# The scores of a chunked recurrence on TensorE, from 128-wide tiles to 32-wide blocks side by side

## The chip, the cores and the metric

The kernel runs on one core of a Trainium2 chip. The core has TensorE (PE in the profile; its loads of the stationary operand are PEld), VectorE (DVE), ScalarE (ACT), GpSimd (POOL) and SyncE (SP), which issues most of the DMAs. The metric is the device time of one execution in microseconds (us): the median of the runs shown.

## The reference, cut to what matters

One layer of a diffusion backbone works on 1024 latent and 128 context tokens: a feed-forward half step, a token mixer (attention beside a gated linear recurrence, HGRN2), and a second feed-forward half step. The recurrence has 8 heads of 64 key and 64 value channels and runs in both directions. Its score matrix is what the change is about:

```python
b = jnp.cumsum(logf.reshape(B, n, CHUNK, H, DK), axis=2)
diff = b[:, :, :, None] - b[:, :, None, :]
decay = jnp.where(mask, jnp.exp(jnp.where(mask, diff, 0.0)), 0.0)
A = jnp.einsum('bntshk,bnthk,bnshk->bnhts', decay, qc, kc)
o_intra = jnp.einsum('bnhts,bnshv->bnthv', A, vc)
```

A[t, s] is the product of query t and key s, decayed by the gates f of the tokens between them; it is multiplied with the values, and the state that comes in from earlier chunks is added. All inputs and outputs are float32.

## The kernel before, in words

The 1152 tokens (latent and context together) lie along the free dimension, in three column blocks of 384 ("chunks", `CW`), each of three 128-token tiles. The program has five stages one after the other: first feed-forward, the recurrence stage (`hgrn`, line 687), attention, the merge of both, second feed-forward. The stage in question goes from about 878 to 1526 us.

In it, two kinds of work share the engines. The first is projections (`proj_f`, `proj_q`, `proj_v`, `proj_gate`, `proj_sg`): products of the normalised input with 128 columns of `w_in`, each a sum of 24 records of 384 columns into one PSUM bank (tile `mm`, lines 451 to 453: the operands are split in a high and a low part, so each product is done three times). They depend on nothing in the scan of the head at hand. The second is the scan itself, for 8 heads by 3 chunks, 24 times:

- `scan_pre` (line 769) makes, on ScalarE, VectorE and GpSimd, decayed keys and queries within groups of 8 tokens (Kb, Qb) and over groups of 8 (KE, QP), with the products T of the gates. Partitions 0 to 63 hold the forward direction (A in the code), 64 to 127 the backward one (B).
- `scan_lev` (line 816) makes the scores. First, line 838: for each 128-token tile Kb times Qb, 64 partitions deep, once per direction, into two PSUM banks of 128 x 3 x 128. VectorE copies from them, under a mask that leaves the 8 x 8 blocks on the diagonal (forward: upper triangle, backward: lower one), into A1 and A2 (`copy_predicated`, line 839). Then four levels m = 8, 16, 32, 64: line 853 multiplies the half-zeroed keys kr with QP, 128 partitions deep, for all pairs of tokens in the 128-token tile; of these only the pairs in neighbouring blocks of m tokens are wanted. Levels 8, 16 and 32 take them with a mask into A1 (line 868), level 64 with two copies on ScalarE (lines 870 and 871). After each level's product KE and QP are multiplied in place with the neighbour's T (line 864; two of QP's halves on VectorE and GpSimd), and ScalarE makes the next half-zeroed keys (lines 844 and 845). At the end VectorE adds A1 and A2 to Af (line 875), TensorE transposes KE (kt, line 879), ScalarE copies that (kT, line 881), and one more product makes dS.
- `scan_out` (line 889), once per head, passes the state through nine tiles on VectorE (line 896) and multiplies Af with the values and QP with the states (po, lines 904 and 908).

Three PSUM banks go round for the scores (tag `lv`), three for small tiles (`sm`), two for the projections (`mm`). A masked copy writes nothing where the mask is zero, and A1 and A2 are zeroed once at the start, so outside the blocks they stay zero.

What sets the order: `hgrn` steps generators by turns. After each `yield` of the level generator one step of projection work (12 records of 384 columns) and one step of the next chunk's `scan_pre` follow, so in TensorE's queue a level's product stands, then 12 projection records, then the next level's product. Each engine works its own instructions in the fixed order that results when the kernel is built. An instruction that waits holds up all that is behind it on its engine.

A float32 product of TensorE stands in the profile as two records; a product of the split operands (fp32r) as one.

Of the kernel before, what the change touches and what calls it, by code (L numbers as in the profile page):

```python
# [9 lines left out]
F32 = mybir.dt.float32  # L10
F32R = mybir.dt.float32r
BF16 = mybir.dt.bfloat16
U8 = mybir.dt.uint8
# [6 lines left out]
P = 128  # L20
# [13 lines left out]
EPS = 1e-6  # L34
SIDE = (1, 2, 3, 4, 5, 6, 7, 8)
QKS = 96.0 ** -0.5
LB_MIN = 1e-8
QW = T // 4
QUARTERS = [(q * QW, (q + 1) * QW) for q in range(4)]
# [48 lines left out]
class Trunk:  # L88
# [494 lines left out]

    def mixer_consts(self, cp):
        nc, a = self.nc, self.a
        self.mask = cp.tile([P, 5, P], U8, name="mask")
        mf = self.tt(F32, "maskf")[:, : 5 * P]
        nc.scalar.dma_start(mf, a["mask"])
        nc.vector.tensor_copy(self.mask.rearrange("p a b -> p (a b)"), mf)
        self.onesb = cp.tile([P, P], F32, name="onesb")  # L590
        nc.vector.memset(self.onesb, 0.0)
        nc.vector.memset(self.onesb[0:64, 0:64], 1.0 / 64)
        nc.vector.memset(self.onesb[64:128, 64:128], 1.0 / 64)
        self.onesq = cp.tile([P, P], F32, name="onesq")
        nc.vector.memset(self.onesq, 1.0 / 384)
        self.onesk = cp.tile([P, P], F32, name="onesk")
        nc.vector.memset(self.onesk, 1.0 / 256)
# [89 lines left out]
    def hgrn(self):  # L687
        nc = self.nc
# [4 lines left out]
        A, B = slice(0, 64), slice(64, P)  # L693
        self.kr = {m: [f32(f"kr{m}_{i}", [P, CW]) for i in range(1)] for m in (8, 16, 32, 64)}
        self.XY = [f32(n, [P, 48, 8]) for n in "XY"]
        self.A1 = [f32(f"A1_{i}", [P, 3, P]) for i in range(2)]
        self.A2 = [f32("A2", [P, 3, P])]
        for m in self.kr:
            for t in self.kr[m]:
                nc.vector.memset(t, 0.0)  # L700
# [115 lines left out]
    def scan_lev(self, d, b):  # L816
# [8 lines left out]
            nc.sync.dma_start(S[A, 0], self.a["state"][d["h"], 0])  # L825
            nc.sync.dma_start(S[B, 7], self.a["state"][d["h"], 1])
        dS = d["dS"]
        A1, A2 = self.A1[self.cnt % 2], self.A2[0]
        self.cnt += 1
        Kb, Qb, KE, Tm = d["pre"]  # L830
        bc = lambda t, m: t.unsqueeze(2).to_broadcast([t.shape[0], t.shape[1], m])
        qp = QP[:, c0 : c0 + CW]
        lv = lambda: self.pp.tile([P, 3, P], F32, tag="lv", bufs=3, name="lv")
        mb = lambda i: self.mask[:, i].unsqueeze(1).to_broadcast([P, 3, P])
        for r, dst, mi in ((A, A1, 0), (B, A2, 1)):
            ps = lv()
            for j in range(3):
                nc.tensor.matmul(ps[:, j], Kb[r, ts(j, P)], Qb[r, ts(j, P)], start=True, stop=True)
            nc.vector.copy_predicated(dst, mb(mi), ps)
        hm = lambda t, m: t.rearrange("p (n h m) -> p n h m", h=2, m=m)  # L840

        def key_half(m):
            kr = self.kr[m][0]
            nc.scalar.copy(hm(kr, m)[A, :, 0], hm(KE, m)[A, :, 0])
            nc.scalar.copy(hm(kr, m)[B, :, 1], hm(KE, m)[B, :, 1])

        key_half(8)
        yield
        for li, m in enumerate((8, 16, 32, 64)):
            kr = self.kr[m][0]  # L850
            ps = lv()
            for j in range(3):
                nc.tensor.matmul(ps[:, j], kr[:, ts(j, P)], qp[:, ts(j, P)], start=True, stop=True)  # L853
            tv = Tm.rearrange("p (n h) -> p n h", h=2)
            tL, tR = tv[:, :, 0], tv[:, :, 1]
            Tn = Gall[:, 3 * b : 3 * b + 3] if m == 64 else tmp(f"T{2 * m}", 3, (P, CW // (2 * m)))
# [8 lines left out]
            nc.vector.tensor_mul(Tn, tL, tR)  # L865
            if m < 64:
                key_half(2 * m)
                nc.vector.copy_predicated(A1, mb(2 + li), ps)
            else:
                nc.scalar.copy(A1[A, :, B], ps[A, :, B])  # L870
                nc.scalar.copy(A1[B, :, A], ps[B, :, A])
            Tm = Tn
            yield
        Af = tmp("Af", 4, (P, 3, P))
        nc.vector.tensor_add(Af, A1, A2)
        d["As"][b] = Af
        pt = self.pp.tile([P, 3, P], F32, tag="sm", bufs=3, name="kt")
        for j in range(3):
# [870 lines left out]
def mask_table():  # L1749
    import numpy as np  # L1750

    s, t = np.arange(P)[:, None], np.arange(P)[None, :]
    same = lambda b: s // b == t // b
    m = [same(8) & (s <= t), same(8) & (s >= t)]
    m += [same(2 * b) & ~same(b) for b in (8, 16, 32)]
    return np.concatenate(m, 1).astype(np.float32)


# [33 lines left out]
```

## Time and profile before

| | |
|---|---|
| median of 3 runs | 3015.09 us (3014.46 to 3016.74) |
| profiled execution, its own time | 3016.44 us |
| its span, first to last instruction | 3014.5 us |
| mean granted TensorE clock | 0.985 |
| TensorE busy, whole span | 2901.7 us (96%) |
| recurrence stage, 878 to 1526 us: TensorE busy | 619.5 of 648 us |
| the same: VectorE busy | 479.0 us |
| the same: ScalarE busy | 338.8 us |
| the same: GpSimd busy | 202.1 us |

Rows of a group read: line, engine, operation, tile written <- tiles read, shapes, how often | busy us, mean ns of one | idle time of the engine just ahead of them, and who ended it. On TensorE a shape such as 128\*32 gives the part of the array that is used: 128 partitions deep, 32 columns wide. Rows of a timeline or a chain read: start in us, length in us, engine, line, operation. A matmul's record reaches from its issue to the end of its drain, so records overlap; the distance from start to start is what counts. A row of waits reads: engine, line, who waits <- for whom: us in total, times, longest.

### The profile page before, as it was taken

What the parts mean: (1) busy time and instruction counts of PE and PEld (TensorE: products, weight loads), DVE (VectorE), ACT (ScalarE), POOL (GpSimd) and SP (SyncE); (2) the same over time, 40 slices, a digit from 0 to 9 for tenths busy, and PEclk for the clock granted to TensorE, in tenths of its full rate; (3) what the DMA queues carried; (4) which work ended last, traced back from release to release, by engine and by line L of the source; (5) the groups of instructions that cost most, each with busy time, mean ns of one, the idle gap of its engine ahead of it and who ended that gap; (6) DMA issues with size and microseconds to landing.
All of it is one profiled execution on the core that took longest, in us unless ns stands there. A gap on an engine that the chain in (4) does not pass through costs nothing.

```text
span 3014.5 us, 49640 instructions
## 1 busy us (share of the span) xinstructions
PE 2901.7 (96%) x18630; PEld 2746.8 (91%) x18630; DVE 1998.2 (66%) x4074; ACT 1238.7 (41%) x2372; POOL 1082.1 (36%) x980
## 2 busy tenths in 40 slices
PE   7999999999989999999998999989999999999998
PEld 5999999999979989898997787669999999999997
DVE  7787777566667777878356777745674665546665
ACT  5432332221364555555245777721362323232113
POOL 3133223453253333333244444532342232236424
PEclk9999999999989999999998999999999999999999
DMA  6643333631111111111110001273352322236211
GB/s 231 204 143 121 124 124 108 247 101 59 62 58 58 38 46 37 51 37 53 58 46 12 18 16 32 63 237 105 106 185 95 101 89 78 76 102 215 90 44 63
DMA packets 148591, 281.34 MB, mean 93 GB/s; under 512 B 18880, under 2 KB 83328, under 8 KB 148352
## 3 DMA queue, kind: packets, MB, share of 16 engines
q1 hardware_dynamic: 148208, 277.85, 28.0%
q8 instruction: 147, 2.41, 0.3%
q14 instruction: 92, 0.75, 0.1%
q10 hardware_dynamic: 144, 0.33, 0.0%
HBM read 214.59 MB, written 63.52 MB: 92 GB/s over the span
## 4 chain that ended last, share of the span: by engine, by line
PE 53%; DVE 11%; ACT 4%; issue 2%; POOL 1%; DMA 1%; DVEq 0%; SPq 0%; ACTq 0%; POOLq 0%
PE b L1546 14%; PE dn L452 4%; PE dn L451 4%; PE dn L453 4%; PE mm L451 4%; PE mm L452 3%; PE mm L453 3%; PE mps L1222 1%; DVE KE L864 1%; PE lv L853 1%; PE ups L453 1%; PE ups L452 1%; PE ups L451 1%; PE sps L1263 1%; PE sps L1265 1%
## 5 line engine op out<-in xcount | busy, mean ns | idle before, releaser
L480 DVE SCALAR_TENSOR_TENSOR x<-dn,modt,x 128x256 f32<-128x256 f32 (+4 forms) x728 | 353.4, 505 | 210.6 <-PE dn L453 209.4
L1546 PE MATMUL b<-xo,wo 128*128 128x288 f32 x3552 | 485.1, 296 | 0.0
L1546 PEld LDWEIGHTS b<-xo,wo 128*128 128x128 f32 x3552 | 477.0, 188 | 0.0
L232 POOL TENSOR_TENSOR wl<-raw,wh 128x1024 fp32r<-128x1024 f32 (+3 forms) x107 | 242.3, 2265 | 371.5 <-ACT wh L231 357.3
L451 PE MATMUL mm<-xh,wh 128*128 128x384 f32 (+1 forms) x1008 | 361.9, 359 | 11.0 <-DVE q L645 8.9
L1546 PE MATMUL b<-bh,wo 128*128 128x288 f32 x1776 | 365.9, 295 | 1.1 <-ACT et L1556 1.1
L453 PE MATMUL mm<-xh,wl 128*128 128x384 f32 (+1 forms) x1008 | 343.0, 340 | 1.8 <-POOL wl L232 1.8
L452 PE MATMUL mm<-xl,wh 128*128 128x384 f32 (+1 forms) x1008 | 342.5, 340 | 0.0
L1546 PEld LDWEIGHTS b<-bh,wo 128*128 128x128 f32 x1776 | 289.2, 188 | 1.3 <-ACT et L1556 1.3
L1546 PE MATMUL b<-bl,wo 128*128 128x288 f32 x888 | 262.0, 295 | 0.0
L451 PEld LDWEIGHTS mm<-xh,wh 128*128 128x128 f32 (+1 forms) x1008 | 190.8, 189 | 20.3 <-DVE q L645 9.7
L1521 ACT CAST wo<-raw 128x512 fp32r<-128x512 f32 x185 | 114.7, 621 | 228.4 <-PE b L1546 112.8
L231 ACT CAST wh<-raw 128x1024 fp32r<-128x1024 f32 (+3 forms) x109 | 105.3, 968 | 251.0 <-PE dn L452 162.0
L451 PE MATMUL dn<-hh,wh 128*128 128x384 f32 (+2 forms) x576 | 195.9, 340 | 1.9 <-DVE et L1562 0.9
L453 PE MATMUL dn<-hh,wl 128*128 128x384 f32 (+2 forms) x576 | 194.4, 337 | 1.0 <-POOL wl L232 1.0
L452 PE MATMUL dn<-hl,wh 128*128 128x384 f32 (+2 forms) x576 | 194.5, 338 | 0.0
L1522 DVE TENSOR_TENSOR wo<-raw,wo 128x512 fp32r<-128x512 f32 x185 | 127.1, 688 | 101.4 <-ACT wo L1521 98.0
L453 PEld LDWEIGHTS mm<-xh,wl 128*128 128x128 f32 (+1 forms) x1008 | 190.4, 189 | 3.1 <-POOL wl L232 2.1
L452 PEld LDWEIGHTS mm<-xl,wh 128*128 128x128 f32 (+1 forms) x1008 | 191.2, 190 | 1.8 <-issue 0.4
L1624 POOL TENSOR_TENSOR hl<-hr,hh 128x1152 fp32r<-128x1152 f32 x44 | 118.1, 2689 | 201.3 <-ACT hh L1623 121.4
L1517 POOL TENSOR_TENSOR ws<-raw 128x256 f32<-128x256 f32 x74 | 66.2, 915 | 301.4 <-DMA raw<-in_w 277.3
L1272 POOL TENSOR_TENSOR ehl<-e,ehl 128x512 fp32r<-128x512 f32 x93 | 123.0, 1327 | 143.0 <-ACT ehl L1270 80.1
(382 smaller groups left out, 7257.0 us busy)
## 6 DMA issues: line engine op xcount, KB each, us to landing
raw<-in_w SPq DMA_DIRECT2D x148, 256.0 KB, 3.1
raw<-in_w SPq DMA_DIRECT2D x58, 512.0 KB, 3.7
hr<-hs SPq DMA_DIRECT2D x44, 576.0 KB, 5.0
hs<-et SPq DMA_DIRECT2D x148, 144.0 KB, 1.8
raw<-in_w_in SPq DMA_DIRECT2D x41, 512.0 KB, 3.6
wada<-in_w_aT SPq DMA_DIRECT2D x80, 256.0 KB, 2.8
wada<-in_w_ada SPq DMA_DIRECT2D x32, 512.0 KB, 5.8
hb<-hd SPq DMA_DIRECT2D x44, 288.0 KB, 3.5
```

What stands on the lines that cost most here:

```text
L231: pin(self.nc.scalar.copy(wh, raw))
L232: pin((eng or self.nc.gpsimd).tensor_sub(wl, raw, wh))
L451: nc.tensor.matmul(ps, wh, xh, start=start and i == 0, stop=False)
L452: nc.tensor.matmul(ps, wh, xl, start=False, stop=False)
L453: nc.tensor.matmul(ps, wl, xh, start=False, stop=stop and i == n - 1)
L480: nc.vector.scalar_tensor_tensor(self.x[m][:, a:b], ps[:, a - lo : b - lo], self.modt[:, gm, m, s : s + 1], self.x[m][:, a:b], ALU.mult, A ...
L1272: eng.tensor_sub(el, e, eh)
L1517: nc.gpsimd.tensor_tensor(o[:, c], x[:, c], y[:, c], op)
L1521: nc.scalar.copy(wh, src[i])
L1522: nc.vector.tensor_sub(wl, src[i], wh)
L1546: nc.tensor.matmul(ps, w[:, k], x[:, k, :QW], start=first, stop=last, skip_group_check=home != i)
L1624: nc.gpsimd.tensor_sub(hl, raw, hh)
```

## The change

The scores are made and masked in 32-token blocks instead of 128-token tiles.

- The first products and levels 8 and 16 are made for 32 x 32 blocks alone: key block g of tile j with query block g, with the result at partitions 32g to 32g+31 of the j-th 32 columns of a compact bank of 128 x 3 x 32. The instruction names a tile of the array by row and column (`tile_position`), so block g uses column strip g, and in the first products the two directions use the two row halves.
- The masked copies, A1, A2 and the masks shrink from 128 x 3 x 128 to 128 x 3 x 32. Level 32 has no masked copy any more. A2 gets a second buffer.
- Levels 32 and 64 go straight to their places in one full bank (128 x 3 x 128), level 32 as four 32 x 32 products per tile (block g of the keys with the neighbouring block of the queries), level 64 as two 64 x 64 products.
- The blocks on the diagonal are put into the same bank with products by the identity: for A1, then A2, and each strip g, 32 columns of the identity times all of A1 (96 columns), the second added onto the first in PSUM. One ScalarE copy of the bank makes Af, in place of two ScalarE copies and the addition on VectorE.

So per chunk 18 products of 128 columns (6 first, 12 for levels) become 24, 12, 12 and 12 of 32 columns, 6 of 64 and 8 of 96.

```diff
@@ -34,6 +34,7 @@
 EPS = 1e-6
 SIDE = (1, 2, 3, 4, 5, 6, 7, 8)
 QKS = 96.0 ** -0.5
+BK = 32
 LB_MIN = 1e-8
 QW = T // 4
 QUARTERS = [(q * QW, (q + 1) * QW) for q in range(4)]
@@ -583,8 +584,8 @@
 
     def mixer_consts(self, cp):
         nc, a = self.nc, self.a
-        self.mask = cp.tile([P, 5, P], U8, name="mask")
-        mf = self.tt(F32, "maskf")[:, : 5 * P]
+        self.mask = cp.tile([P, 4, BK], U8, name="mask")
+        mf = self.tt(F32, "maskf")[:, : 4 * BK]
         nc.scalar.dma_start(mf, a["mask"])
         nc.vector.tensor_copy(self.mask.rearrange("p a b -> p (a b)"), mf)
         self.onesb = cp.tile([P, P], F32, name="onesb")
@@ -693,8 +694,8 @@
         A, B = slice(0, 64), slice(64, P)
         self.kr = {m: [f32(f"kr{m}_{i}", [P, CW]) for i in range(1)] for m in (8, 16, 32, 64)}
         self.XY = [f32(n, [P, 48, 8]) for n in "XY"]
-        self.A1 = [f32(f"A1_{i}", [P, 3, P]) for i in range(2)]
-        self.A2 = [f32("A2", [P, 3, P])]
+        self.A1 = [f32(f"A1_{i}", [P, 3, BK]) for i in range(2)]
+        self.A2 = [f32(f"A2_{i}", [P, 3, BK]) for i in range(2)]
         for m in self.kr:
             for t in self.kr[m]:
                 nc.vector.memset(t, 0.0)
@@ -825,17 +826,27 @@
             nc.sync.dma_start(S[A, 0], self.a["state"][d["h"], 0])
             nc.sync.dma_start(S[B, 7], self.a["state"][d["h"], 1])
         dS = d["dS"]
-        A1, A2 = self.A1[self.cnt % 2], self.A2[0]
+        A1, A2 = self.A1[self.cnt % 2], self.A2[self.cnt % 2]
         self.cnt += 1
         Kb, Qb, KE, Tm = d["pre"]
         bc = lambda t, m: t.unsqueeze(2).to_broadcast([t.shape[0], t.shape[1], m])
         qp = QP[:, c0 : c0 + CW]
-        lv = lambda: self.pp.tile([P, 3, P], F32, tag="lv", bufs=3, name="lv")
-        mb = lambda i: self.mask[:, i].unsqueeze(1).to_broadcast([P, 3, P])
-        for r, dst, mi in ((A, A1, 0), (B, A2, 1)):
-            ps = lv()
-            for j in range(3):
-                nc.tensor.matmul(ps[:, j], Kb[r, ts(j, P)], Qb[r, ts(j, P)], start=True, stop=True)
+        lv = lambda n=BK: self.pp.tile([P, 3, n], F32, tag="lv", bufs=3, name="lv")
+        mb = lambda i: self.mask[:, i].unsqueeze(1).to_broadcast([P, 3, BK])
+        blk = lambda j, g, n=BK: slice(j * P + g * n, j * P + g * n + n)
+
+        def tiles(out, lhsT, rhs, row, col, start=True, stop=True):
+            nc.tensor.matmul(
+                out, lhsT, rhs, start=start, stop=stop, tile_position=(row, col), skip_group_check=True
+            )
+
+        first = lv(), lv()
+        for j in range(3):
+            for g in range(4):
+                for r, ps in zip((A, B), first):
+                    v = blk(j, g)
+                    tiles(ps[ts(g, BK), j], Kb[r, v], Qb[r, v], r.start, BK * g)
+        for ps, dst, mi in zip(first, (A1, A2), (0, 1)):
             nc.vector.copy_predicated(dst, mb(mi), ps)
         hm = lambda t, m: t.rearrange("p (n h m) -> p n h m", h=2, m=m)
 
@@ -846,11 +857,19 @@
 
         key_half(8)
         yield
+        full = None
         for li, m in enumerate((8, 16, 32, 64)):
             kr = self.kr[m][0]
-            ps = lv()
+            if m < BK:
+                ps, n, far = lv(), BK, 0
+            else:
+                ps = full = full or lv(P)
+                n, far = m, 1
             for j in range(3):
-                nc.tensor.matmul(ps[:, j], kr[:, ts(j, P)], qp[:, ts(j, P)], start=True, stop=True)
+                for g in range(P // n):
+                    q = g ^ far
+                    out = ps[ts(g, n), j] if not far else ps[ts(g, n), j, ts(q, n)]
+                    tiles(out, kr[:, blk(j, g, n)], qp[:, blk(j, q, n)], 0, n * g)
             tv = Tm.rearrange("p (n h) -> p n h", h=2)
             tL, tR = tv[:, :, 0], tv[:, :, 1]
             Tn = Gall[:, 3 * b : 3 * b + 3] if m == 64 else tmp(f"T{2 * m}", 3, (P, CW // (2 * m)))
@@ -865,14 +884,15 @@
             nc.vector.tensor_mul(Tn, tL, tR)
             if m < 64:
                 key_half(2 * m)
+            if m < BK:
                 nc.vector.copy_predicated(A1, mb(2 + li), ps)
-            else:
-                nc.scalar.copy(A1[A, :, B], ps[A, :, B])
-                nc.scalar.copy(A1[B, :, A], ps[B, :, A])
             Tm = Tn
             yield
+        for i, t in enumerate((A1, A2)):
+            for g in range(4):
+                tiles(full[ts(g, BK), :, ts(g, BK)], self.ident[:, ts(g, BK)], t, 0, BK * g, not i, bool(i))
         Af = tmp("Af", 4, (P, 3, P))
-        nc.vector.tensor_add(Af, A1, A2)
+        nc.scalar.copy(Af, full)
         d["As"][b] = Af
         pt = self.pp.tile([P, 3, P], F32, tag="sm", bufs=3, name="kt")
         for j in range(3):
@@ -1749,10 +1769,10 @@
 def mask_table():
     import numpy as np
 
-    s, t = np.arange(P)[:, None], np.arange(P)[None, :]
+    s, t = np.arange(P)[:, None] % BK, np.arange(BK)[None, :]
     same = lambda b: s // b == t // b
     m = [same(8) & (s <= t), same(8) & (s >= t)]
-    m += [same(2 * b) & ~same(b) for b in (8, 16, 32)]
+    m += [same(2 * b) & ~same(b) for b in (8, 16)]
     return np.concatenate(m, 1).astype(np.float32)
 
 
```

The order on TensorE at the end of a chunk, before: the product of level 64 (kr\_0\_8912 are that level's keys), then projection records, then the transposes kt.

```order
L853 MATMUL lv<-QP,kr_0_8912 128x128 x3
L451 MATMUL mm<-xh_8318,wh 128x384
L452 MATMUL mm<-xl_8319,wh 128x384
L453 MATMUL mm<-xh_8318,wl 128x384
L451 MATMUL mm<-xh_8320,wh 128x384
L452 MATMUL mm<-xl_8321,wh 128x384
L453 MATMUL mm<-xh_8320,wl 128x384
L879 MATMUL kt<-ident,KE 128x128 x3
L451 MATMUL mm<-xh_8322,wh 128x384
```

And after the change, the same place (A\_0\_8915 is A1, A\_0\_8917 is A2):

```order
L454 MATMUL mm<-xh_8318,wl 128x384
L452 MATMUL mm<-xh_8320,wh 128x384
L839 MATMUL lv<-QP,kr_0_8912 64x64 x6
L453 MATMUL mm<-xl_8321,wh 128x384
L454 MATMUL mm<-xh_8320,wl 128x384
L839 MATMUL lv<-A_0_8915,ident 32x3x32 x4
L839 MATMUL lv<-A_0_8917,ident 32x3x32 x4
L899 MATMUL kt<-ident,KE 128x128 x3
L452 MATMUL mm<-xh_8322,wh 128x384
```

The level's three products have become six on 64-column strips, and eight identity products stand right ahead of the transposes; the level's product stands some projection records later than it did.

The order on VectorE around levels 32 and 64 of a chunk, before (KE, QP and T as above; X, Y, TK, TQ belong to the next chunk's `scan_pre`):

```order
L645 TENSOR_TENSOR q<-mm,sg 128x384
L864 TENSOR_TENSOR QP<-QP,T_10326 64x6x32
L868 COPY_PREDICATED A_0_8915<-mask,lv 128x384
L864 TENSOR_TENSOR KE<-KE,T_10550 64x6x32 x2
L790 TENSOR_TENSOR X<-fs,X 128x48
L803 COPY TK<-Y 64x48
L806 TENSOR_TENSOR TQ<-Y,fs 64x48
L791 RECIPROCAL Y<-X 128x48x3
L864 TENSOR_TENSOR QP<-QP,T_10355 64x3x64
L875 TENSOR_TENSOR Af<-A_0_8915,A_8917 128x384
L864 TENSOR_TENSOR KE<-KE,T_10577 64x3x64 x2
```

And after the change:

```order
L883 TENSOR_TENSOR QP<-QP,T_10572 64x6x32
L646 TENSOR_TENSOR q<-mm,sg 128x384
L883 TENSOR_TENSOR KE<-KE,T_10848 64x6x32 x2
L791 TENSOR_TENSOR X<-fs,X 128x48
L804 COPY TK<-Y 64x48
L807 TENSOR_TENSOR TQ<-Y,fs 64x48
L792 RECIPROCAL Y<-X 128x48x3
L883 TENSOR_TENSOR QP<-QP,T_10610 64x3x64
L883 TENSOR_TENSOR KE<-KE,T_10884 64x3x64 x2
```

The masked copy of level 32 and the addition are gone; a step of a projection (q) stands behind the multiplication of QP where it stood ahead of it.

## The prediction

> **What bounds the kernel now.** I read the page first, then the recurrence stage alone (the stretch from 878 to 1526 us, in which every instruction of the change lies) by busy time, by groups, by waits and by the chain that ended last, and last the timeline around single bursts.
>
> The page's head, then the row of the busy-time table for that stretch (PE, PEld, VectorE, ScalarE, GpSimd, granted clock):
>
> ```profile
> span 3014.5 us, 49640 instructions
> ...
> 878.00:1526.00 648.00, 619.47 (x3883) 584.00 (x3882) 479.01 (x1050) 338.76 (x702) 202.13 (x236) 0.99 0.15 48
> ```
>
> TensorE is the bound in the stage, 619 of 648 us at a granted clock of 0.99. But 648 - 619 = 28 us are open, and the waits of TensorE and of its weight loads there say on whom (us in total, times, longest):
>
> ```profile
> PE lv L853 <- DVE QP L864: 16.9, 14, 2.3
> PE lv L853 <- POOL QP L864: 4.0, 5, 1.2
> PEld lv L853 <- POOL QP L864: 8.2, 13, 1.5
> ```
>
> After each level's score product the query copy QP is multiplied in place (VectorE and GpSimd, L864), and the next level's product needs it. These waits are 21 us on TensorE, 29 us with the weight loads. So there are two ways to gain: less work on TensorE, or an earlier QP. The chain between 1193 and 1360 us (two heads) shows when QP is late: it runs on VectorE and ScalarE from 1234 to 1275 and from 1289 to 1334, 86 of about 156 us, and on TensorE otherwise. The pieces of it that the change touches:
>
> ```profile
> 1235.31 0.59 DVE A L868
> ...
> 1242.42 0.56 DVE Af L875
> ...
> 1252.63 0.54 DVE A L839
> ...
> 1254.39 0.44 DVE A L839
> ...
> 1256.60 0.58 DVE A L868
> ...
> 1260.55 0.58 DVE A L868
> ...
> 1264.28 0.59 DVE A L868
> ...
> 1295.33 0.58 DVE A L868
> ...
> 1300.54 0.56 DVE Af L875
> ...
> 1306.21 1.06 DVE A L839 x2
> ...
> 1310.48 0.49 DVE A L868
> ...
> 1313.25 0.58 DVE A L868
> ...
> 1317.02 0.58 DVE A L868
> ...
> 1320.64 0.56 DVE Af L875
> ...
> 1327.81 0.98 DVE A L839 x2
> ```
>
> The first seven sum to 3.88 us, the other eight to 5.39: 9.3 us of chain for two heads.
>
> **The change, part by part.** Six groups of the stage carry the prices (busy us, mean ns of one):
>
> ```profile
> L853 PE MATMUL lv<-QP,kr 128*128 128x128 f32 x576 | 83.7, 282 | 21.0 <-DVE QP L864 16.9 <-POOL QP L864 4.0
> L868 DVE COPY_PREDICATED A<-mask,lv 128x384 f32<-128x384 uint8 x72 | 42.6, 592 | 2.1
> L839 DVE COPY_PREDICATED A<-mask,lv 128x384 f32<-128x384 uint8 x48 | 25.4, 577 | 68.8 <-PE lv L838 68.5
> L875 DVE TENSOR_TENSOR Af<-A,A 128x384 f32<-128x384 f32 x24 | 15.1, 629 | 1.7 <-ACT A L871 1.5
> L870 ACT COPY A<-lv 64x192 f32<-64x192 f32 x24 | 7.4, 310 | 11.6 <-PE lv L853 11.4
> L881 ACT COPY kT<-kt 128x384 f32<-128x384 f32 x24 | 11.5, 478 | 9.5 <-PE kt L879 9.4
> ```
>
> There are 24 chunks (8 heads by 3). One f32 product is two records: 24 x 4 levels x 3 = 288 products stand as x576.
>
> *VectorE.* A chunk has 2 x 0.577 + 3 x 0.592 + 0.629 = 3.56 us of masks and adding. After it has four masked copies of 96 columns. No such copy is in the trace; from below it is bounded by a two-column copy out of PSUM, from above by the 0.59 us of 384 columns:
>
> ```profile
> L167 DVE COPY bias<-pb x2: 147/153/159, 67.1 to 70.6; 128x2 f32<-128x2 f32 x2
> ```
>
> Between the two, (592 - 153)/382 = 1.15 ns a column: 0.153 + 94 x 1.15 ns = 0.26 us. I take that. So 3.56 becomes 1.04, and 2.5 us a chunk, 60 us in all, leave VectorE. If a copy cost what it costs now, 3.56 - 4 x 0.59 = 1.2 us a chunk, 29 us, would still go; at 0.153 a copy it would be 71.
>
> *ScalarE.* Two copies of 0.31 go, one of 128x384 out of PSUM comes, priced by the kT row: 0.62 becomes 0.48 us. The new copy waits for the identity products; behind it on ScalarE stands the kT copy, which waits for the transposes right behind those products anyway. So it costs nothing while that order holds, and 0.48 us a chunk, 11 us, if ScalarE were the bound. The identity products in turn wait for masks that VectorE finished two levels earlier, and the score bank that they share with levels 32 and 64 is held until that copy, with two other banks left for the next chunk's first products.
>
> *TensorE, before.* Two bursts with their neighbours:
>
> ```profile
> 1206.27 0.34 PE L453 MATMUL mm<-xh,wl 128*128 128x384 f32 x1
> 1206.45 0.83 PE L853 MATMUL lv<-QP,kr 128*128 128x128 f32 x6
> ...
> 1207.29 0.34 PE L452 MATMUL mm<-xl,wh 128*128 128x384 f32 x1
> ...
> 1202.74 0.38 PE L908 MATMUL po<-QP,S 128*64 128x128 f32 x2
> 1203.05 1.26 PE L838 MATMUL lv<-Qb,Kb 64*128 64x128 f32 x12
> 1204.24 0.44 PE L451 MATMUL mm<-xh,wh 128*128 128x384 f32 x1
> 1204.52 0.34 PE L452 MATMUL mm<-xl,wh 128*128 128x384 f32 x1
> ```
>
> A projection record of 384 columns takes 0.18 us (1206.45 - 1206.27). The row of 1207.29 is the second such record behind the level's burst, which so costs 1207.29 - 1206.45 - 0.18 = 0.66 us, 0.11 per record. The first burst, split in two row halves, costs 1204.52 - 1202.74 - 2 x 0.11 - 0.18 = 1.38 us. A chunk has 1.38 + 4 x 0.66 = 4.0 us of scores.
>
> *TensorE, after.* 18 products become 74 (24, 12, 12, 12, 6 and 8), 36 records 148, in six bursts, each on an array cut in columns. The trace has one such burst, the four modulation products side by side:
>
> ```profile
> 1989.93 0.30 PE L451 MATMUL ups<-oh,wh 128*128 128x288 f32 x1
> 1990.07 0.29 PE L452 MATMUL ups<-ol,wh 128*128 128x288 f32 x1
> 1990.29 0.64 PE L250 MATMUL adap<-wada,sc 128*32 128x256 f32 x8
> ...
> 1991.09 0.30 PE L451 MATMUL ups<-oh,wh 128*128 128x288 f32 x1
> ...
> 1990.28 0.16 PEld L250 LDWEIGHTS adap<-wada,sc 128*32 128x32 f32 x8 [0.16 <-issue]
> ...
> L250 PEld LDWEIGHTS adap<-wada,sc x256: 105/109/156, 6.4 to 2042.8; 128*32 128x32 f32 x128
> ```
>
> Three things are in it. Eight records of 256 columns, which one after another would take 8 x 0.22 = 1.7 us (0.11 for 128 columns), end in 0.64: the four column tiles run at once. Eight weight loads of 0.107 start within 0.16 - 0.107 = 0.05 us: one record is issued every 7 ns. And the burst costs more than it streams: 1991.09 - 1990.07 = 1.02, less two slots of ups (1990.07 - 1989.93, 0.13 to 0.14) and two streams of 0.22 in a tile, leaves 0.31 to 0.33 us for emptying and refilling the array.
>
> I price six bursts at 0.33 = 1.98 us, and the streams by the slower of issue (7 ns) and the longest tile (a 32-column record a quarter of 0.11, 0.028 us): first 48 x 7 ns = 0.33; three levels of 24 records, six to a tile, 0.17 each; level 64, six of 64 columns to a tile, 0.33; identity products, four of 96 columns to a tile, 0.34. Together 1.5 us, and 3.5 with the bursts, against 4.0: 0.5 us less a chunk, 12 us less in all. Lower end: every record at 7 ns, 1.04 + 1.98 = 3.0, 24 us less. Upper end: no overlap at this size: 48 + 72 = 120 records at 0.028, 12 at 0.055 and 16 at 0.083 are 5.3 us, 7.3 with the bursts, 79 us more. I take the first, since the only burst with several column tiles shows them overlapping.
>
> A rule of the Trainium skill speaks against: "TensorEngine Tiling (Array Packing)", section Performance Considerations, under Instruction Overhead, gives each matmul some 60 cycles of overhead however few columns it moves, and warns against taking a tiling factor from a dimension that is already small. At the 2.4 GHz that "TensorE: Matmul & The Clock Gate" gives in its opening table that is 25 ns a record as an estimate, 3.7 us of streams a chunk and about 40 us more on TensorE than now. No row here has 32 moving columns on column tiles, so the trace doesn't decide it; the row of 256 columns can't show it.
>
> *What of it reaches the end.* On the chain of two heads, the first stretch has two L839, four L868 and one Af. Two of three L868 stay, so 3.88 becomes (2 + 2.7) x 0.26 = 1.2; the second has four L839, four L868, two Af, 5.39 becomes (4 + 2.7) x 0.26 = 1.7. That is 6.4 us for two heads, 25 for eight, and no more than the 21 to 29 us that TensorE waits can come back. But ScalarE's pieces and GpSimd's own QP step stay on that chain, so I take 15. TensorE's 12 us count only where the chain runs on it, 70 of 156 us: 5. Sum: 20 us less. With the cover gone (TensorE dearer than now) QP is early by itself, and what is then late is only TensorE.
>
> The profiled run took 3016.44 us, 1.9 more than its span and 1.4 more than the median of 3015.09. 3016.4 - 20 = 2996.4, which on the median's scale is 2995.
>
> **Rivals.**
> *The relief is swallowed.* GpSimd's multiplication of QP (L864) starts only after the level's product, and nothing in the change shortens it; ScalarE's pieces stay too. For it: 12 of the 29 us of waits name GpSimd. Against it: GpSimd is ready early where VectorE hands it Qb and TQ early. Then 0 to 6 us come back, TensorE's own gain goes into the waits: 3011.
>
> *Bursts that don't overlap (slower).* If 32-column records leave TensorE one by one in all six bursts, it pays 79 us more and no longer waits for QP (29 less): 3065. If they overlap in part, at the quarter-record spacing only for issue, 148 x 0.028 = 4.1 us a chunk, 2.1 more than now: 50 - 25 = 25 us more, 3040. This is the case that the Trainium skill's rule on overhead ("TensorEngine Tiling (Array Packing)", Performance Considerations) would bring about. It decides from the point at which a chunk's streams take (12 + 15)/24 = 1.1 us more than priced, so about 18 ns a record on average where I have 10. For it: nothing so short is in the trace, and the first burst's two row halves are independent today, and its 12 records still take 1204.24 - 1203.05 = 1.19 us, where six slots of 0.11 would be 0.66, so halves don't overlap in full. Against it: the 7 ns.
>
> *Everything counts.* VectorE's 25 us on the chain come back whole and TensorE's 12 too: 37 less, 2979. Against it: the two are the same open 28 us in good part.
>
> *Not what it says.* That the masks aren't smaller can't be: the copies' own columns fall from 384 to 96, and the order shows four a chunk and no adding.
>
> **How the numbers follow.** The forecast, 2995, gets 0.56; everything counts 0.08; swallowed 0.14; bursts that don't overlap 0.22. A difference of 0.2%, 6 us, is what the measurement tells from none. So faster 0.64, same 0.14, slower 0.22. The forecast alone spans 2980 to 3008 (5 to 11 us of TensorE's own, 8 to 25 of waits). The range reaches down to 2972, past 2979, and up to 3042, which takes in the partly overlapping bursts and leaves the whole of 3065 out, about 0.12, with 0.04 below.
>
> **What would show it.** In the stage's groups: masked copies of 128x96 at about 0.26 us, x96, and VectorE's busy time near 420 us instead of 479. In the timeline: six bursts a chunk, the first of 48 records in about 0.7 us with its entry and exit, levels of 24 in about 0.5. In the waits: PE on DVE QP down from 16.9 to under 8 us. Score bursts that take 1 us and more, a stage longer than 648 us with no wait on QP left, would be the slower rival; shorter masks with the same waits, now ended by GpSimd or ScalarE, the swallowed one. I am wrong if the stage ends later than 1526 us though the masks are short.

## The result, and the profile after

The changed kernel takes 2985.78 us (2985.39 to 2990.49, 4 runs) against 3015.25 us before (3014.46 to 3016.74, 4 runs): a ratio of 0.9903, 95% interval 0.9891 to 0.9915, or 29 us less. The forecast was 2995 with a range of 2972 to 3042.

The head of its page and the busy times of the stage (PE, PEld, VectorE, ScalarE, GpSimd, granted clock), first of the kernel after, then of the kernel before. Each row runs from the stage's first projection records to the sums `ops` behind its last head, which comes some 10 us ahead of the 1526 us used so far:

```profile
span 2983.6 us, 54969 instructions
...
838.00:1484.00 646.00, 618.00 (x6650) 554.61 (x6649) 438.09 (x1029) 348.38 (x715) 221.44 (x253) 0.99 0.16 52
```

```profile
840.00:1516.00 676.00, 638.22 (x3961) 601.29 (x3962) 488.87 (x1075) 355.37 (x738) 222.01 (x253) 0.98 0.16 49
```

The stage is 30 us shorter, which is the whole difference: TensorE is busy 20 us less in it and idle 10 us less (28 instead of 38). VectorE is busy 51 us less. The groups that took the place of the masks and the addition (busy us, mean ns of one | idle ahead):

```profile
L888 DVE COPY_PREDICATED A<-mask,lv 128x96 f32<-128x96 uint8 x48 | 12.9, 268 | 1.5
...
L895 ACT COPY Af<-lv 128x384 f32<-128x384 f32 x24 | 11.5, 477 | 18.0 <-PE lv L839 18.0
L850 DVE COPY_PREDICATED A<-mask,lv 128x96 f32<-128x96 uint8 x48 | 10.1, 258 | 71.8 <-PE lv L839 71.5
```

23.0 us of masked copies stand where 83.1 us of copies and addition stood. The waits of the stage (us in total, times, longest):

```profile
PE mm L452 <- DVE q L646: 9.1, 2, 4.7
...
PE lv L839 <- DVE QP L883: 7.0, 9, 1.6
...
PE dS L905 <- ACT kT L901: 5.8, 3, 1.9
...
PEld lv L839 <- POOL QP L883: 3.7, 8, 0.9
```

TensorE's wait on VectorE's QP fell from 16.9 to 7.0 us, that on GpSimd's QP (4.0) is gone from PE. A new one is there, dS on ScalarE's kT, 5.8 us. The bursts of one chunk with their neighbours:

```profile
1261.98 0.38 PE L928 MATMUL po<-QP,S 128*64 128x128 f32 x2
1262.30 0.62 PE L839 MATMUL lv<-Qb,Kb 64*32 64x32 f32 x48
...
1263.13 0.34 PE L453 MATMUL mm<-xl,wh 128*128 128x384 f32 x1
...
1270.19 0.34 PE L454 MATMUL mm<-xh,wl 128*128 128x384 f32 x1
1270.46 0.40 PE L839 MATMUL lv<-QP,kr 128*32 128x32 f32 x24
...
1271.07 0.33 PE L453 MATMUL mm<-xl,wh 128*128 128x384 f32 x1
...
1272.81 0.34 PE L454 MATMUL mm<-xh,wl 128*128 128x384 f32 x1
1273.08 0.57 PE L839 MATMUL lv<-QP,kr 128*64 128x64 f32 x12
...
1273.86 0.34 PE L453 MATMUL mm<-xl,wh 128*128 128x384 f32 x1
...
1275.60 0.34 PE L454 MATMUL mm<-xh,wl 128*128 128x384 f32 x1
1275.87 0.54 PE L839 MATMUL lv<-A,ident 128*32 128x96 f32 x16
1276.34 0.55 PE L899 MATMUL kt<-ident,KE 128*128 128x128 f32 x3
...
1276.90 0.34 PE L453 MATMUL mm<-xl,wh 128*128 128x384 f32 x1
```

Read from the last record ahead to the second projection record behind, less the slots of those two records (0.18 each, 0.22 for the two of po): first burst 1263.13 - 1261.98 - 0.22 - 0.18 = 0.75; levels 8 to 32, 1271.07 - 1270.19 - 0.36 = 0.52; level 64, 0.69; identity products 1276.90 - 1275.60 - 0.36 = 0.94 with the transposes, 0.61 without the 0.33 of their three records. A chunk has 0.75 + 3 x 0.52 + 0.69 + 0.61 = 3.6 us of score bursts, where it had 4.0: about 10 us less in all.

So of the 30 us, 10 are TensorE's own work, as forecast. Most of the other 20 are waits, though TensorE's idle time fell by 10 only: a projection record counts as busy for 0.34 us where its slot is 0.18, so at each burst up to 0.16 us of waiting stands as busy. Read by slots, the level bursts that stand between projection records lasted 30 us longer in sum than the shortest of their kind before (90 bursts), and 10 us longer after (93). The granted clock in the stage differs a little as well (0.982 before, 0.987 after, about 3 us). The experiments ask what made the waits go: VectorE's relief, the shorter bursts, or something else.

### The profile page after: what moved, and what is told of

The parts are those of the page before. It is cut to its first block, busy times and chain, and to the rows that moved or that the text cites. A ratio compares the mean times of both kernels' runs of the same rounds, so it can differ in the third digit from the quotient of the medians.

```text
span 2983.6 us, 54969 instructions
## 1 busy us (share of the span) xinstructions
PE 2878.1 (96%) x21318; PEld 2698.5 (90%) x21318; DVE 1946.1 (65%) x4027; ACT 1231.8 (41%) x2348; POOL 1082.7 (36%) x980
```

## The experiments

In the table, "QP wait" is TensorE's wait on VectorE's QP in the stage, in one profile; the ratio is to runs of the kernel before taken alongside, whose median lay between 3014.55 and 3016.5 us. The profiles of e2 and e10 had a lower granted clock from 878 to 1526 us than the others (0.98 and 0.97, else 0.99 or 1.00), so their waits stand beside the others with less weight.

| run | time, us | ratio, 95% | QP wait |
|---|---|---|---|
| before | 3015.25 | 1 | 16.9 |
| after | 2985.78 | 0.9903 [0.9891, 0.9915] | 7.0 |
| e1 short masks alone | 3010.45 | 0.9978 [0.9969, 0.9988] | 22.3 |
| e2 after, masks at full cost | 3012.48 | 0.9986 [0.9977, 0.9996] | 21.1 |
| e3 after, one strip at a time | 3005.29 | 0.9960 [0.9946, 0.9975] | 2.5 |
| e4 after, identity in level 64 | 2988.98 | 0.9905 [0.9891, 0.9920] | 18.0 |
| e5 e4, state pass held back | 2985.87 | 0.9900 [0.9886, 0.9915] | 15.3 |
| e6 e1, state pass held back | 3014.62 | 0.9995 [0.9986, 1.0004] | 14.8 |
| e7 before, state pass held back | 3017.39 | 1.0008 [0.9999, 1.0018] | 14.8 |
| e8 before, wl in four pieces | 3012.72 | 0.9994 [0.9985, 1.0004] | 15.9 |
| e9 e1 in the order of after | 2992.61 | 0.9923 [0.9909, 0.9938] | 3.1 |
| e10 after in the order of e1 | 3020.72 | 1.0016 [1.0005, 1.0027] | 31.5 |
| e11 e4 in the order of after | 2981.55 | 0.9888 [0.9872, 0.9905] | 6.5 |
| e12 before in the order of after | 3004.76 | 0.9968 [0.9954, 0.9982] | 4.2 |

### The halves, one at a time (e1, e2)

e1 is the kernel before with masked copies of 96 columns; level 32 is not copied, Af is a ScalarE copy of level 64's bank, and A2 has its second buffer.

```diff
-            nc.vector.copy_predicated(dst, mb(mi), ps)
+            nc.vector.copy_predicated(dst[:, :, :32], mb(mi), ps[:, :, :32])
...
-                nc.vector.copy_predicated(A1, mb(2 + li), ps)
+            if m < 32:
+                nc.vector.copy_predicated(A1[:, :, :32], mb(2 + li), ps[:, :, :32])
...
-        nc.vector.tensor_add(Af, A1, A2)
+        nc.scalar.copy(Af, ps)
```

> The kernel before with VectorE's part of the change alone: 128-wide products on TensorE as before, but the masked copies take only the first 32 columns of each tile (four a chunk, 128x96), level 32 is not copied at all, and Af is one ScalarE copy of level 64's bank in place of two copies and the VectorE addition. So the parts of the scores outside those columns, and the sum, are left out. Theory A (two gains that add: bursts 10.6 us shorter on TensorE, and some 20 of 30 us of waits for QP that come back because VectorE has 55 us less): bursts as before, waits as after, so 3015 - 20 = 2995 us, 2990 to 3000. Rival B (the waits shrink because the bursts are short and the level products come earlier; the masks matter little): 3010 to 3015.

Measured: 3010.45 us. VectorE got its relief (422 us busy from 878 to 1526 us, 479 before), and TensorE waited for QP no less (16.9 us before):

```profile
878.00:1526.00 648.00, 620.46 (x3902) 587.75 (x3901) 422.24 (x1005) 335.37 (x678) 201.30 (x237) 0.99 0.15 49
```

```profile
PE lv L853 <- DVE QP L864: 22.3, 18, 2.1
```

e2 is the other half: the changed kernel, with each compact copy written four times over and two more operations of 384 columns on spare data, so that VectorE pays what it paid before (85.1 us for these groups, 83.1 before).

```diff
-            nc.vector.copy_predicated(dst, mb(mi), ps)
+            nc.vector.copy_predicated(dst, mb(mi), b4(ps))
...
+            elif m == BK:
+                nc.vector.copy_predicated(self.pad[B]..., pm, late)
...
+        nc.vector.tensor_add(pv, late, late)
```

> The changed kernel with its bursts, but VectorE as loaded as in the kernel before: the four masked copies write each compact block four times (384 columns out of PSUM), and two operations of 384 columns on spare data stand where level 32's masked copy and the addition stood. Theory A: TensorE's 10.6 us stay gained, the waits for QP return: 2986 + 20 = 3006 us; up to 3013 if the shorter bursts are eaten by the late QP where the chain runs on VectorE. Rival B: 2986 to 2992.

Measured: 3012.48 us, 21.1 us of QP waits. So one half gives 7 us, the other 4, both together 29. My sum, which added the halves, had no place for that. But neither run measures its half alone: each is a build of its own, and its instructions come in an order of their own. On VectorE 551 pairs that stand less than 40 places apart are the other way round in e1 than in the kernel before, and 662 in e2 than in the changed kernel. The runs e9 to e12 take this up.

### The price of the bursts (e3, e4)

e3 issues each burst strip by strip, so that records in a row use the same strip.

```diff
-            for j in range(3):
-                for g in range(P // n):
+            for g in range(P // n):
+                for j in range(3):
```

> The changed kernel with the same products in another order within the first and the level bursts: strip by strip (all three 128-token tiles of one column strip, then the next strip; the two row halves one after the other), so that neighbours in the queue share a strip. If strips overlap only when neighbours differ, first bursts go from 0.75 to about 1.7 us, levels from 0.52 to 1.0, level 64 from 0.70 to 1.0: 2.7 us a chunk, 65 us: 3050. If TensorE looks ahead over one strip's six records, about half: 3015. If issue alone (9 ns a record) sets the bursts, nothing changes: 2986.

Measured: 3005.29 us. A level of 24 records takes 1279.72 - 1278.60 - 0.36 = 0.76 us instead of 0.52:

```profile
1278.60 0.34 PE L454 MATMUL mm<-xh,wl 128*128 128x384 f32 x1
1278.87 0.65 PE L839 MATMUL lv<-QP,kr 128*32 128x32 f32 x24
1279.44 0.44 PE L452 MATMUL mm<-xh,wh 128*128 128x384 f32 x1
1279.72 0.33 PE L453 MATMUL mm<-xl,wh 128*128 128x384 f32 x1
```

The first burst takes 1.13 us instead of 0.75 and level 64 0.86 instead of 0.69. Over all bursts of a chunk it is 1.3 us, 31 us for TensorE, about the half that the middle expectation had. Some 17 of them reach the time (0.9960 - 0.9903); of the rest, waits for QP (7.0 to 2.5 us) and for kT (5.8 to 3.9) give back some 6, and where the others went was not followed up. The weight loads of a level show the price, first here, then in the changed kernel:

```profile
1278.87 0.53 PEld L839 LDWEIGHTS lv<-QP,kr 128*32 128x32 f32 x24 [0.25 <-issue]
```

```profile
1270.46 0.28 PEld L839 LDWEIGHTS lv<-QP,kr 128*32 128x32 f32 x24 [0.25 <-issue]
```

A load lasts 0.11 us, so 24 of them start within 0.42 us here and 0.17 there: 18 ns and 7.4 ns a record. Strips overlap in part even so: in single records, starts 27 to 32 ns apart alternate with starts 1 to 4 ns apart.

e4 puts the identity products into level 64's burst (level 64 in 32-column strips too), one burst less a chunk.

```diff
-                n, far = m, 1
+                n, far = BK, m // BK
...
+            if m == 64:
+                for i, t in enumerate((A1, A2)):
+                    for g in range(4):
+                        tiles(full[ts(g, BK), :, ts(g, BK)], self.ident[:, ts(g, BK)], t, 0, BK * g, not i, bool(i))
```

> The changed kernel with one burst less a chunk: level 64 is made in four 32-column strips of 64 moving columns (same array cut as the identity products), and the identity products follow right behind it, ahead of the projection records that stood between. If each entry and exit of a cut array costs 0.33 us as priced: 24 x 0.33 = 8 us less, 2978 us. If the cost goes with the records or with each product's own latency: 2984 to 2987. If the identity products now wait for a mask that isn't ready: more than 2986.

Measured: 2988.98 us, no better than the changed kernel. The burst itself was 0.3 us cheaper, 7.5 us over 24 chunks (its rows stand at e11), but the QP waits rose from 7 to 18 us. TensorE had less to do and waited more: the same puzzle as in e1, VectorE having had less to do there.

### One place, and one neighbour (e5 to e8)

In e4 the last chunk of every second head takes 34.6 us from first burst to first burst, in the changed kernel 31. At that place VectorE waits for dS with the state pass S, which then runs 2.31 us where the others of its kind take 0.3. Two rows of e4, VectorE and GpSimd (the bracket is the idle time ahead and who ended it):

```profile
1229.10 2.31 DVE L918 SCALAR_TENSOR_TENSOR S<-S,Gall,dS 64x64 f32<-64x64 f32 x1 [1.74 <-ACT dS L908]
```

```profile
1228.93 2.40 POOL L233 TENSOR_TENSOR wl<-raw,wh 128x1024 fp32r<-128x1024 f32 x1 [2.56 <-ACT wh L232]
```

The second theory was that this S was the cause. e5, e6 and e7 hold S in VectorE's queue behind the QP of level 32, in e4, e1 and the kernel before:

```diff
-        for j in range(7):
+        with self.tc.issue_after(d["hold"]):
+            for j in range(7):
```

> Kernel: the one with the identity products in level 64's burst (2988.98 us), and the state pass S of scan_out held in VectorE's queue behind the QP multiplication of level 32 of the head's last chunk; nothing else. Theory O (order in VectorE's queue): in that kernel the last chunk of every second head takes 34.5 us instead of 31.3, since an S there waits 1.7 us for dS ahead of the reciprocals of the next chunk, runs 2.3 us beside GpSimd's wl, and so makes the first level's QP late by 2.7 us. Held back, that goes: the four chunks fall to about 31.5, DVE QP waits from 18 to under 9 us, time about 2977 (2972 to 2982). Rival T (the shorter bursts themselves leave QP late): waits stay at 15 to 18 us, 2985 to 2990.

> Kernel: before.py with 96-column masked copies alone (3010.45 us; it leaves out parts of the scores and the sum as that one does), and the same hold on S. Theory O: VectorE's relief was worth more than the 5 us that it showed, and the S that waits for dS took it back; the four chunks of 34.5 us fall to about 31.8, the waits on DVE QP from 22 to about 10, time about 2999 (2995 to 3003). Rival T (without shorter bursts VectorE's relief is worth little): 3007 to 3012.

> Kernel: before.py with the same hold on S and nothing else. Theory O: in the kernel before VectorE is busy without a gap ahead of that place, S there is only 1.0 us of a 4 us backlog, so 1 to 4 us come back: 3011 to 3015, DVE QP waits 13 to 17 us. If the place of S alone were the whole cause, the chunks of 35.6 us would fall to 32 and the time to about 3003.

Measured: 2985.87, 3014.62 and 3017.39 us, that is 0.1% less, 0.2% more and 0.1% more than without the hold; only e6's difference is clear of noise. The theory fell. In e6 the QP waits fell from 22.3 to 14.8 us, but the level products then waited 8.3 us for T. In e5 the chunk still takes 34.7 us: with S gone, the next instruction in VectorE's queue waits, now for ScalarE's X, and is drawn out beside wl in its turn (two of them in the row):

```profile
1227.29 2.49 DVE L791 TENSOR_TENSOR X<-fs,X 128x48 f32<-128x48 f32 x2 [1.96 <-ACT X L789]
```

e8 asks about wl alone, in the kernel before: GpSimd makes it in four pieces.

```diff
-        pin((eng or self.nc.gpsimd).tensor_sub(wl, raw, wh))
+        for k in range(0, shape[1], step):
+            ks = slice(k, k + step)
+            pin((eng or self.nc.gpsimd).tensor_sub(wl[:, ks], raw[:, ks], wh[:, ks]))
```

> Kernel: before.py with GpSimd's low parts of the w_in weights (wl, 128x1024 in 2.4 us) made in four pieces of 256 columns; the result is the same. Theory G: a VectorE operation that starts while GpSimd makes wl ends only with that instruction (21 VectorE operations of the stage take 2.3 to 2.9 us where they take 0.2 to 1.0 elsewhere); with pieces of 0.6 us such an operation takes 1.2 us at most, VectorE's busy time falls by 15 to 30 us, the DVE QP waits from 17 to about 8 to 12 us, time 3003 to 3010. Rival: the long durations belong to something else (a wait inside the instruction, the order) and stay, 3014 to 3016; or the sharing is by bandwidth, then the long operations are as many in sum, only spread.

Measured: 3012.72 us, no difference that can be told, with VectorE's instructions in the same order as before. VectorE operations of over 1.8 us in the stage fell from 21 to 8, but seven of these 8 last longer than they did (3.17 to 3.34 us, 2.76 to 2.91 before). The busy times from 840 to 1526 us, first of e8, then of the kernel before (columns as above):

```profile
840.00:1526.00 686.00, 648.34 (x4023) 610.06 (x4024) 496.87 (x1087) 365.86 (x750) 243.00 (x364) 0.99 0.15 49
```

```profile
840.00:1526.00 686.00, 648.22 (x4018) 611.29 (x4019) 494.79 (x1087) 365.23 (x751) 224.15 (x255) 0.98 0.16 49
```

VectorE's did not fall at all, and GpSimd's rose by 19. The time lies nearer the rivals' 3014 to 3016 than theory G's 3003 to 3010, and the blocked time is only spread, as the second rival said; its reason, a shared bandwidth, is not shown.

### The order of the queues (e9 to e12)

What e1, e4 and the changed kernel also differ in is the order in which instructions stand in the queues. That order is laid out when the kernel is built, and comes out differently when instructions change. The changed kernel and e1 have the same 1029 instructions on VectorE in the stage; 701 pairs of them that stand less than 40 places apart are the other way round, on ScalarE 235, on GpSimd 28, while TensorE's score bursts stand at the same places but for three. e4 and the changed kernel differ in 212 pairs on VectorE and 145 on ScalarE; e3, whose waits vanished, has the order of the changed kernel but for 60 pairs.

So these four runs keep every instruction and fix the order. Once the stage is laid out, the instructions of TensorE, VectorE, ScalarE and GpSimd are tied to one another, engine by engine, in the order of the other kernel (an order of issue, no wait; the issues of transfers stay free):

```diff
+        for x, y in zip(seq, seq[1:]):
+            self.tc.add_manual_dep(y, x.name, info(), reason="set order")
```

> Kernel: before.py with 96-column masked copies alone (3010.45 us; it leaves out parts of the scores and the sum as that one does), its instructions unchanged, but the order in the queues of TensorE, VectorE, ScalarE and GpSimd in the recurrence stage fixed to the one that the changed kernel has (its VectorE has the same 1029 instructions there). Theory O: in the changed kernel the queues were laid out anew along with the bursts, QP ahead of q and of the next chunk's reciprocals; that order gives back the waits, so this kernel comes to the changed kernel's time plus the 10.6 us of TensorE's dearer bursts: 2996 (2993 to 3000), waits on DVE QP under 12 us. Rival D (the shorter bursts themselves free QP earlier, the order only follows): 3008 to 3014, waits 18 us and more. In between (2000 of both): each has a share, read off by where it falls.

Measured: 2992.61 us, just below the range of theory O (the "2000 of both" in the expectation can't be right; between its two ranges lie 3000 to 3008 us). Without one instruction changed, e1 in the order of the changed kernel is 17 us faster (0.9978 - 0.9923), and the QP waits fell from 22.3 us to:

```profile
PE lv L1082 <- DVE QP L1093: 3.1, 3, 1.0
```

In the traces, e9, e11 and e12 have not one of the pairs left that stood the other way round than in the changed kernel on VectorE, ScalarE and GpSimd. A place shows how the order works. In e1 (first fence, VectorE's timeline; second, TensorE's) the QP of a level stands behind a reciprocal that belongs to the next chunk, which waits 1.23 us for GpSimd's Y; the level's burst then waits 1.54 us for QP:

```profile
1153.50 0.56 DVE L799 TENSOR_TENSOR Qb<-qx,X 64x384 f32<-64x384 f32 x1
1155.29 1.35 DVE L793 RECIPROCAL X<-Y 128x192 f32<-128x192 f32 x1 [1.23 <-POOL Y L790]
1156.67 0.35 DVE L864 TENSOR_TENSOR QP<-QP,T 64x192 f32<-64x192 f32 x1
```

```profile
1157.18 0.91 PE L853 MATMUL lv<-QP,kr 128*128 128x128 f32 x6 [1.54 <-DVE QP L864]
```

At the same place in e9 QP stands ahead of that reciprocal, the level's burst waits for nothing, and the reciprocal falls one level later, where its input is there:

```profile
1145.59 0.56 DVE L1028 TENSOR_TENSOR Qb<-qx,X 64x384 f32<-64x384 f32 x1
1146.07 0.56 DVE L1093 TENSOR_TENSOR QP<-QP,T 64x192 f32<-64x192 f32 x1
...
1147.96 1.35 DVE L1022 RECIPROCAL X<-Y 128x192 f32<-128x192 f32 x1
```

```profile
1147.89 0.83 PE L1082 MATMUL lv<-QP,kr 128*128 128x128 f32 x6
```

(Line numbers differ, since the table of the order stands in the file.)

> Kernel: the changed kernel, its instructions unchanged, with the order in the four queues fixed to that of the kernel with 96-column masked copies and the old bursts. Theory O: QP stands behind q and the reciprocals again, the waits come back to 18 us and more, and the time is that kernel's 3010.45 less TensorE's 10.6: about 3000 (2996 to 3003). Rival D: the order makes no difference, 2984 to 2990, waits on DVE QP 7 to 10 us.

Measured: 3020.72 us. The changed kernel in the order of e1 has lost all of its gain, and more than expected (3000):

```profile
PE lv L1070 <- DVE QP L1114: 31.5, 20, 3.3
```

The profile is of the slowest of its ten executions (3030.55 us), at a lower granted clock:

```profile
878.00:1526.00 648.00, 602.51 (x6523) 538.55 (x6523) 410.65 (x990) 326.57 (x668) 196.10 (x233) 0.97 0.15 48
```

> Kernel: the one with the identity products in level 64's burst (2988.98 us), its instructions unchanged, in the order that the changed kernel has in the four queues (the identity products stay in level 64's burst). Theory O: its own order made QP late (18 us of waits); in the changed kernel's order they fall to 10 or less and TensorE's 7.5 us show: 2975 to 2981. Rival D: 2985 to 2990, as before.

Measured: 2981.55 us, QP waits of 6.5 us. This is the fastest version measured, 34 us under the kernel before; against the changed one its 4 us are within the noise, against e4, which has the same instructions, it is 5 us faster by the ratios, also not clear of noise, with 11.5 us less of QP waits. Its joint burst costs 1272.17 - 1270.82 - 0.36 = 0.99 us where two took 0.69 + 0.61:

```profile
1270.82 0.34 PE L660 MATMUL mm<-xh,wl 128*128 128x384 f32 x1
1271.09 0.54 PE L1070 MATMUL lv<-QP,kr 128*32 128x64 f32 x24
1271.44 0.51 PE L1070 MATMUL lv<-A,ident 128*32 128x96 f32 x16
...
1272.17 0.34 PE L659 MATMUL mm<-xl,wh 128*128 128x384 f32 x1
```

> Kernel: before.py with all its instructions, with the order in the four queues fixed to that of the changed kernel; what the changed kernel has not (the masked copy of level 32 right behind that level's QP, the two ScalarE copies of level 64 and the addition, which are left free) is added. It leaves nothing out. Theory O in full (the order alone is what the waits hang on): the waits on DVE QP fall under 8 us and the time is that of the 96-column masks in this order, 2992.6, or a little more: 2990 to 2998. Theory O with room (that order only holds while VectorE has the room that the short masks give): 67 us more on VectorE bring part of the waits back, 2999 to 3008. Rival (the order is worth nothing without the change): 3012 to 3020.

Measured: 3004.76 us. The kernel before, complete and with its long masks, in the order of the changed kernel, is 0.3% faster, as the expectation "with room" had it:

```profile
PE mm L655 <- DVE q L849: 12.4, 5, 7.5
PE dS L1114 <- ACT kT L1110: 10.1, 3, 3.4
PE lv L1082 <- DVE QP L1093: 4.2, 5, 1.0
```

Its QP waits are nearly gone, but others are longer than in the changed kernel (q 12.4 against 9.1, kT 10.1 against 5.8). VectorE's long masks may show there, but e11 waits 11.4 us for q without them, so that is not shown.

In the order of the changed kernel the steps now go in one direction, ratio by ratio, each difference times 3015 us: order alone 1 - 0.9968, 10 us; VectorE's relief 0.9968 - 0.9923, 14 us; shorter bursts 0.9923 - 0.9903, 6 us; one burst less (e11) 0.9903 - 0.9888, 5 us. By the intervals of the table the first carries an uncertainty of some 4 us and the others of some 6, so order and relief are clear of noise, and the last two are not. e9 also leaves out a ScalarE copy that e12 has and gives A2 a second buffer. In the order of e1 the same bursts bring nothing: from e1 to e10 the time rises by 11 us. No run ties a kernel in its own order, so what the tying itself does is not measured; but tied kernels came out 17 us faster (e9) and 34 us slower (e10) than the same instructions untied, so it can't be the whole effect.

## Why the prediction was right, and where it was not

The time lay in the range and on the side forecast; the gain was 29 us where I had 20.

- *VectorE's price*: right. 0.263 us a masked copy on average (forecast 0.26), 60.1 us of work gone (60). VectorE's busy time fell by 51, not 60, since some operations that run beside GpSimd's wl are drawn out, and others than before: S took 46.0 us where it took 33.3, and one step of T (128x12) 18.5 where it took 4.4, while KE took 75.4 where it took 86.2.
- *TensorE's price*: right. 3.6 us of bursts a chunk (3.5), 10 us less in all (12). The first burst 0.75 (0.7), the levels 0.52 (0.5). The weight loads part the two terms. In a level 24 loads start 7.4 ns apart (e3's section), which leaves 0.52 - 24 x 0.0074 = 0.34 us for entry and exit (7 ns and 0.33). In the first burst 48 loads of 0.11 us start within 0.51 us, 8.6 ns apart, and leave 0.75 - 48 x 0.0086 = 0.34:

```profile
1262.29 0.51 PEld L839 LDWEIGHTS lv<-Qb,Kb 64*32 64x32 f32 x48 [0.17 <-issue]
```

- *The slower rival*, bursts that don't overlap: its condition, about 18 ns a record on average, was not met: a chunk's bursts without six times 0.34 are 1.6 us, 11 ns a record. The Trainium skill's rule that spoke for it ("TensorEngine Tiling (Array Packing)", Performance Considerations, Instruction Overhead: some 60 cycles a matmul however short) does not hold for these records: 7.4 to 8.6 ns is well under the 25 estimated from it. With records in a row on one strip (e3) it is 18 ns, still under it.
- *ScalarE costs nothing while that order holds*: the condition was named and not priced. The order did not hold: dS now waits 5.8 us for kT. In the rows of ScalarE ahead of one such wait the kT copy stands behind the cast of a weight, a projection's sigmoid, Af and two fs:

```profile
1224.16 1.05 ACT L232 CAST wh<-raw 128x1024 fp32r<-128x1024 f32 x1
1225.12 0.48 ACT L624 ACTIVATE sg<-mm 128x384 f32<-128x384 f32 x1
1225.50 0.47 ACT L895 COPY Af<-lv 128x384 f32<-128x384 f32 x1
1225.86 1.44 ACT L636 ACTIVATE fs<-sg,lb,lb 64x384 f32<-64x384 f32 x2
1227.32 0.48 ACT L901 COPY kT<-kt 128x384 f32<-128x384 f32 x1
```

- *What of it reaches the end*: this step failed, though its sum came near. I took 15 us of waits out of VectorE's shorter chain and 5 of TensorE's 12. Measured in the new order, VectorE's relief is worth 14 and the bursts 6, each give or take 6 us, which agrees with these two terms. But they hold only in that order: from the kernel before to e1, relief and another order together gave 7, and in the order of e1 the bursts gave nothing. The missing term is the order of the queues itself, 10 us with no instruction changed (e12). That the build came out in a good order was luck: the same instructions in the order of e1 (e10) take 3020.72 us, longer than the kernel before. I had looked at the new order at two places, had seen QP step ahead of q on VectorE, and gave it no price.
- *"Everything counts"* (2979, chance 0.08) came closer to the time, but by a sum that the runs do not bear out: it let VectorE's relief bring back 25 us.
- *QP waits under 8 us*: right, 7.0. The reason behind it was half right: e1 has the short masks and waits 22.3.

Open is which of the pairs in the order carry the 10 us: e9 to e12 moved all four queues together, and holding back the one instruction that looked guilty did nothing. Open is also why the changed kernel in the order of e1 is slower than e1 itself, though its bursts are shorter. Its granted clock was lower (0.984 on average over its ten executions, 0.987 over e1's), which over some 3000 us could be up to 9 us; whether the order brings the lower clock is not known.

## What to carry to other kernels

Where queues are laid out anew at each build, a changed instruction moves others, and a comparison of two builds measures both. Fix the order of the one in the other before an effect is put down to the instruction; four such runs showed here what eight edits could not. In a stage where several engines wait for one another in turn, what two builds gave by themselves need not add up (7 and 4 us here, 29 together): see first what stands ahead of the late instruction in its own queue, and what that waits for.

## What the runs showed of the hardware

- Weight loads of short records, issued in turn to separate column strips, start 7.4 ns apart in a burst of 24 and 8.6 ns apart in one of 48, and going into such a burst and out of it costs 0.34 us. Strip by strip 24 of them start 18 ns apart. So the order of issue within a burst is worth 0.24 us for 24 records.
- A VectorE operation that reads two tiles of SBUF can be drawn out until GpSimd's wl ends: S in e4 starts at 1229.10, 0.17 after wl, and ends at 1231.41, 0.08 after wl's end. The Trainium skill states that a VectorE instruction with two SBUF inputs contends with a GpSimd instruction that reads SBUF, through an exclusive lock on shared ports ("SBUF — State Buffer", Who interferes with whom), and this place agrees. e8 adds that shorter GpSimd instructions didn't help: fewer VectorE operations are long, but VectorE's busy time stays (497 and 495 us). Seven operations stay drawn out through all four pieces there: X starts at 1108.82, beside GpSimd's QP and ahead of the first piece at 1109.22, and ends at 1112.15, 0.11 after the last piece. Why these don't come in between two pieces is open.
